# Strassen-like pairs in a two-layer encoder: block sums laid side by side, another order of a pair's products, block sums behind evacuations

## The chip, the cores and the metric

The kernel runs on one core of one Trainium2 chip. The metric is the device time of one execution in microseconds. Three runs of the kernel before have a median of 1820.8 us (1817.36 to 1824.54).

## The reference

A trunk of two layers over a sequence of 512 rows with 1024 channels, in float32. Each layer adds half a SwiGLU block, a mixer, and half a SwiGLU block again:

```python
h = _rmsnorm(x, ffn1_norm[layer])
x = x + 0.5 * _swiglu(h, ffn1_w_gate[layer], ffn1_w_up[layer], ffn1_w_down[layer])
...
def _swiglu(h, w_gate, w_up, w_down):
    return (jax.nn.silu(h @ w_gate) * (h @ w_up)) @ w_down
```

The hidden width of a SwiGLU block is 2816. The mixer of the first layer is a state-space mixer beside an S5 scan, that of the second banded attention beside causal pooling. The four SwiGLU blocks (f0 to f3) are most of the work, and the change is in them.

## The kernel before, in words

**Layout and stages.** Channels lie on the 128 partitions, the 512 rows of the sequence on the free axis. The program goes f0, even mixer, f1, f2, odd mixer, f3. Each float32 product is made from split operands: a matrix is split into a rounded part and a rest (`split_steps`, L582: ScalarE writes the rounded part, VectorE the rest), and three products (rounded x rounded, rounded x rest, rest x rounded) add up in one PSUM bank.

**Classic tiles and pairs.** The 22 output tiles of the gate matrix and of the up matrix go two by two (q = 0 to 10). Up to q = 7 in f0, and up to q = 1 in f1, f2 and f3, they are computed one tile after another ("classic"), with an evacuation (`evac`) by VectorE for each. From there on a pair of tiles is computed with seven block products instead of eight, after Winograd's form of Strassen's method (`pair`, L924): six pairs in f0 and 18 in each other stage, 60 in all; one half for the gate matrix (tag gs), one for the up matrix (tag us). A pair needs combinations of its weights (W1, W3, W4, W2; made by the feeder, `feed`, L508, on VectorE as raw<-raw sums and then split into whl and wh) and combinations of the normed activations, the block sums TA and TB (`blocks`, L876). The block sums are made once a stage: four steps, each with two normed tiles, four differences of 256 columns, and two splits into hg tiles.

**The products of a pair.** `block` (L904) runs four contraction steps into one bank. A narrow block has three products of 256 columns per step. A wide block (with TA at hi, or TB) has per step one product of 512 columns, which reads the rounded and the rest part of a block sum in one instruction, and one of 256. The two parts lie 512 elements apart in the tile, since each tile is [rounded 512 | rest 512] and a block takes columns lo (0 to 255) or hi (256 to 511) of both. A pair has three banks: X (W1 with N), Z (W4 with N, then W3 with TA), Y (W3 with TA, then W4 with TB, then W2 with TB). The last block, W2, is run later by `last()`: after the down products that follow the pair, or inside the next pair where none follow (`before`, the first pairs of f1, f2 and f3). Banks come from a pool of four that are used in turn.

**VectorE in a pair.** It reads X as p (p1), adds Y's two halves and p into the result tile (`plus`: gs<-ps,p then gs<-ps,gs), adds Z, and so on. The result tile gs or us is a single buffer: `ftile` (L842) waits until the gate of the tiles before (`gate`, L976: us<-gs,us and two splits) has issued its product. Y's bank gets its second group of products only when `plus` of the first has read it.

**What sets the order.** The order of all instructions is fixed when the program is built, by a planner: `Clock` (L111) keeps an estimated time for each engine and adds the cost of every instruction (`cost`, L145; for VectorE 0.068 us and 1/960 or 1/1920 us per element). Every few products `tick` (L285) offers a step first to urgent work, then to the feeder of weights, then to threads in order of `PRIO` (L58): a step for VectorE is issued when its operands are nearly ready and VectorE's estimated queue is less than BACKLOG beyond now (`on`, L320). Evacuations, gates and block sums have priority 0, the preparation of the S5 tables in f0 has 6. Waiting (`until`, `idle`) goes on ticking with no product issued.

Of the kernel before, what the change touches and what calls it, by code (L numbers as in the profile page):

```python
# [14 lines left out]
PSUM = bass.MemoryType.PSUM  # L15
# [17 lines left out]
for _i, _pools in enumerate(((),(3,),(2,),(1,0))):  # L33
# [21 lines left out]
WARM = 12  # L55
SLACK = {"f0": 1.5, "even": 0.0, "f1": 0.0, "f2": 0.0, "odd": 0.4, "f3": 0.0}
PREP_SLACK = 4.0
PRIO = {"evac": 0, "gate": 0, "small": 5, "prep": 6, "blocks": 0, "s5_bounce": 1, "s5_quarter": 0, "s5_gate": 0, "s5_eighth": 1,  # L58
        "ssd_dt": 1, "conv": 1, "ssd_chunk": 1, "ssd_tail": 0, "z": 2, "qk_norm": 0, "pool": 3, "attn": 2}
LIVE = 3  # L60
CHAINS = 2
# [49 lines left out]
class Clock:  # L111


    def __init__(self):
        self.t = dict.fromkeys(list(ENGINES.values()) + ["RING", "DMA"], 0.0)
        self.t["ACT"], self.t["RING"], self.t["DVE"], self.t["PE"] = 1.9, 0.65, 0.6, 0.95
        self.w, self.r, self.floor, self.stuck = {}, {}, 0.0, 0
        self.lanes, self.born = [0.0] * 8, {}

    @property  # L120
# [24 lines left out]
    def cost(eng, op, out, kw):  # L145
# [12 lines left out]
        ptr = any(hasattr(kw.get(k), "space") for k in ("scalar", "scalar1"))  # L158
        return (0.128 if ptr else 0.068) + n / (1920 if one else 960) * (1 if eng == "DVE" else 2)

    def note(self, eng, op, args, kw):
        out = kw.get("out", args[0] if args else None)
        outs = [out] + ([kw["accum_out"]] if "accum_out" in kw else [])
        ins = [v for k, v in kw.items() if k not in ("out", "accum_out") and hasattr(v, "free_size")]
        dma = op == "dma_start"
        at = self.t["RING"] if dma else self.t[eng]
        for ap in ins:
            for b in self.blocks(ap):
                t, e = self.w.get(b, (0.0, ""))
                at = max(at, t + (0.15 if e != eng else 0.11 if eng != "PE" else 0.0))  # L170
        for ap in outs:
            at = max(at, self.born.get(ap.name, 0.0))
            for b in self.blocks(ap):
                t, e = self.w.get(b, (0.0, ""))
                at = max(at, 0.0 if dma and e == "DMA" else t if e == eng else t + 0.1, self.r.get(b, 0.0))
        if dma and eng == "POOL":
            self.t["POOL"] = max(at, self.t["POOL"]) + 1.1
            end = max(self.t["DMA"], self.t["POOL"] + 1.0) + max(0.18, out.free_size() * out.partition_size() * 4 / 360e3)
            self.t["DMA"] = end
            end += 0.95  # L180
        elif dma:
            at = max(at, self.lanes.pop(0))
            self.t["RING"] = at + 0.48
            end = max(self.t["DMA"], at + 1.1) + max(0.06, out.free_size() * out.partition_size() * 4 / 360e3)
            self.t["DMA"] = end
            end += 1.06
            self.lanes.append(end)
        else:
            end = at + self.cost(eng, op, out, kw)
            self.t[eng] = end  # L190
        for ap in outs:
            for b in self.blocks(ap):
                self.w[b] = (max(end, self.w.get(b, (0.0, ""))[0]), "DMA" if dma else eng)
        for ap in ins:
            for b in self.blocks(ap):
                self.r[b] = max(self.r.get(b, 0.0), end)
# [55 lines left out]
class Builder:  # L252
# [26 lines left out]

    def phase(self, name):  # L280
        self.name = name
        self.backlog, self.guard, self.most = BACKLOG[name], GUARD[name], AHEAD[name]


# [296 lines left out]

    def split_steps(self, src, dst, scale=None):  # L582
        nc = self.nc
        yield from self.on("ACT", src)
# [4 lines left out]
        yield from self.on("DVE", dst[:, 0])  # L589
# [158 lines left out]
    def ffn(self, f, gi, then, prepare=None):  # L748
        nc, tc = self.nc, self.tc
        self.phase(f"f{f}")  # L750
        self.f, self.then, self.final, self.sideb = f, then, False, 2
        h = self.begin_norm(gi)
        with ExitStack() as st:
            self.ft = st.enter_context(tc.tile_pool(name=self.n("ft"), bufs=2))
            ex = ExitStack()
            prep = None
            if prepare is not None:
                prep = prepare(ex.enter_context(tc.tile_pool(name=self.n("prep"), bufs=1)))
# [11 lines left out]
            self.N, self.TA, self.TB = h, [], []  # L770
            grown, pending = False, None
            for key in ffn_items(f):
                if not grown and not self.running(prep) and CLASSIC[f == 0] < NFF // 2:
# [8 lines left out]
                if key[0] != "wgu":  # L782
                    w = self.unit(*key)
                if key[0] == "wgu":
                    m, i = key[2:]
                    if (m % 2, i) == (0, 0):
                        t, done = {"gs": None, "us": None}, []
                    if (m, i) == (0, 0):
                        both = self.proj_tiles([key, ("wgu", f, 0, 1)], h)
                    if m == 0:  # L790
                        ps = both[i]
                    else:
                        w = self.unit(*key)
# [7 lines left out]
                elif key[0] == "pair":  # L801
                    q, i = key[2:]
                    if i == 0:
                        t = {}
                    last = self.pair(w, t, "us" if i else "gs", pending)

                    def pending(last=last, t=t, q=q, i=i):
                        last()
                        if i == 0:
                            nc.scalar.activation(out=t["gs"], in_=t["gs"], func=AF.Silu)  # L810
                        else:
                            self.add("gate", self.gate(t, g, q, [1] * 4, 1))
                            if q == NFF // 2 - 1:
                                self.give(*self.N, *self.TA, *self.TB)
                else:
                    cg, kp = key[2:]
                    grp = next(gr for gr in GROUPS if kp in gr)
                    if kp == grp[0]:
                        pss = [None] * 4
                        if cg == 0 and grp == GROUPS[-1]:  # L820
                            self.tail()
                    self.out_unit(pss, w, g, kp, cg, kp == grp[0], kp == grp[-1], 0.5, "a")
                    self.give(w)
                    if cg == 1:
                        self.give(g[2 * kp], g[2 * kp + 1])
                    if pending:
                        pending()
                        pending = None
# [47 lines left out]
    def blocks(self, h, gi, late):  # L876
# [5 lines left out]
        for kk in range(4):  # L882
# [11 lines left out]
            v.tensor_tensor(out=t4, in0=n2[:, a], in1=t2, op=ALU.subtract)  # L894
            self.give(tn)
            for c, d in ((lo, self.TA), (hi, self.TB)):
                t = yield from self.grab("hg")
                yield from self.split_steps(rt[:, c], t)
                d.append(t)
            self.give(rt)  # L900
        self.xhold, self.reserve = False, 0


    def block(self, ps, t, at, rhs, c, more=False, wide=False):  # L904
        nc = self.nc
        for kk in range(4):
            self.until(lambda: len(rhs) > kk)
            w = slice(at + kk * P, at + kk * P + P)
            r = rhs[kk]
            first, last = kk == 0 and not more, kk == 3  # L910
            o = ps[:, 0:256]
            go = dict(start=first, stop=False, skip_group_check=more)
            if wide:
                nc.tensor.matmul(out=ps.rearrange("p (a b) -> p a b", a=2), lhsT=t[:, 0, w], rhs=r[:, :, c], **go)
            else:
                nc.tensor.matmul(out=o, lhsT=t[:, 0, w], rhs=r[:, 0, c], **go)
                go["start"] = False
                nc.tensor.matmul(out=o, lhsT=t[:, 0, w], rhs=r[:, 1, c], **go)
            nc.tensor.matmul(out=o, lhsT=t[:, 1, w], rhs=r[:, 0, c], start=False, stop=last, skip_group_check=more)
            self.tick()  # L920


# [1 line left out]
    def pair(self, w, t, tag, before):  # L924
        v = self.nc.vector
        W1, W3, W4, W2 = w
# [13 lines left out]
        self.block(X, W1, 0, N[0:4], lo)  # L940
        p1 = new("p1", 2)
        times(p1, X[:, lo], lo)
        Z = self.main_ps()
        self.block(Z[:, hi], W4, 512, N[4:8], hi)
        if before:
            before()
        t[tag] = dst = self.ftile(tag)
        Y = self.main_ps()
        self.block(Y, W3, 512, TA, hi, wide=wide)
        plus(dst[:, 0, hi], Y, p1)  # L950
        self.block(X, W1, 512, N[4:8], lo, more=True)
        self.give(W1)
        times(dst[:, 0, lo], X[:, lo], lo)
        self.free(X)
# [12 lines left out]

        def last():
            self.block(Y, W2, 0, TB, hi, more=True, wide=wide)
            self.give(W2)  # L970
            plus(dst[:, 1, lo], Y, p1)
            self.free(Y)
# [1120 lines left out]
```

## Time and profile before

| | |
|---|---|
| median of three runs | 1820.8 us |
| the profiled execution | 1818.1 us, its span 1816.4 us |
| TensorE products | 10082, busy 99% of the span |
| VectorE | 2902 instructions, busy 84% |
| ScalarE | 1032 instructions, busy 41% |
| granted TensorE clock, mean | 0.999 |

All rows have the same source line, that of a helper which records each operation (L207), so groups are told apart by the tiles they write and read: ps is a PSUM bank, whl and wh are split weights, hg a split activation or block sum, raw an unsplit weight or sum. "A<-B 128x512 xN | busy, mean" is a group of N instructions with its busy time in us and the mean of one in ns; what follows is the idle time of the engine ahead of them and who ended it. PEld is the loading of weights into TensorE, which carries the waits of the product behind it. Products are pipelined: the busy times of neighbours overlap, so the distance of their starts is what one costs.

### The profile page before, as it was taken

The numbers are of one execution on the slowest core, as the hardware profiler recorded it, in microseconds if no ns is written. First come the engines' busy times: TensorE is split into PE (matmuls) and PEld (weight loads), VectorE is DVE, ScalarE is ACT, GpSimd is POOL, SyncE is SP. The second block draws the span as 40 slices with busy tenths as digits, with TensorE's granted clock in tenths as the row PEclk, the third lists the DMA queues.
The fourth block names the chain that finished last, engine by engine and source line by source line (L and its number), as shares of the span: only waits on it lengthen the run. The fifth ranks groups of instructions, "written<-read, shape, count | busy, mean of one in ns | idle before, by whom it ended". The sixth has DMA issues, their size and how long they took to land.

```text
span 1816.4 us, 26183 instructions
## 1 busy us (share of the span) xinstructions
PE 1790.0 (99%) x10082; PEld 1535.7 (85%) x10082; DVE 1518.7 (84%) x2902; ACT 746.4 (41%) x1032; POOL 34.0 (2%) x53
## 2 busy tenths in 40 slices
PE   9999999999999999999999999999999999999999
PEld 7877888878778888888888898988888888988887
DVE  8999878777885899998779998987678679999984
ACT  4224433233584533333354333323466564333331
POOL 0000000000010000000010000000000010000000
PEclk9999999999999999999999999999999999999999
DMA  5256433336674532333343333333325452333331
GB/s 194 88 152 194 130 93 93 116 136 196 173 181 139 127 107 96 101 104 107 126 119 102 105 105 105 105 106 115 111 82 116 129 134 87 105 105 104 106 103 71
DMA packets 83341, 216.57 MB, mean 119 GB/s; under 512 B 18288, under 2 KB 30608, under 8 KB 82064
## 3 DMA queue, kind: packets, MB, share of 16 engines
q1 hardware_dynamic: 78032, 196.52, 33.7%
q0 software_dynamic: 5040, 18.35, 6.0%
q8 instruction: 79, 1.29, 0.3%
q14 instruction: 46, 0.38, 0.1%
q10 hardware_dynamic: 144, 0.02, 0.0%
HBM read 202.26 MB, written 12.60 MB: 118 GB/s over the span
## 4 chain that ended last, share of the span: by engine, by line
PE 64%; DVE 23%; DMA 6%; issue 4%; ACT 3%; SPq 0%; DVEq 0%; ACTq 0%
PE ps L207 64%; DVE whl L207 5%; DVE raw L207 4%; DVE us L207 4%; DMA raw<-in_wgu_dram 3%; ACT whl L207 2%; DVE gs L207 2%; DVE hg L207 2%; DVE x L207 1%; DVE wh L207 1%; DVE p L207 1%; DMA raw<-in_wev_dram 0%; DMA prm<-prm 0%; SPq L207 0%; DMA hg<-s5us 0%
## 5 line engine op out<-in xcount | busy, mean ns | idle before, releaser
L207 PE MATMUL ps<-hg,whl 128*128 128x512 f32 (+1 forms) x8400 | 1596.6, 349 | 12.4 <-DVE gs L207 6.1
L207 PEld LDWEIGHTS ps<-hg,whl 128*128 128x128 f32 x8400 | 1341.3, 189 | 221.4 <-DVE gs L207 10.8
L207 ACT CAST whl<-raw 128x1024 fp32r<-128x1024 f32 x374 | 391.1, 1048 | 500.9 <-PE ps L207 356.1
L207 DVE TENSOR_TENSOR whl<-raw,whl 128x1024 fp32r<-128x1024 f32 x339 | 412.2, 1219 | 100.6 <-ACT whl L207 100.3
L207 DVE TENSOR_TENSOR raw<-raw,raw 128x512 f32<-128x512 f32 (+1 forms) x212 | 129.5, 646 | 2.5
L207 ACT CAST hg<-us 128x512 fp32r<-128x512 f32 x88 | 52.0, 618 | 156.1 <-DVE us L207 155.9
L207 ACT ACTIVATE gs<-gs 128x1024 f32<-128x1024 f32 x44 | 46.6, 1060 | 159.9 <-DVE gs L207 159.9
L207 DVE SCALAR_TENSOR_TENSOR x<-ps,x 128x512 f32<-128x512 f32 x128 | 83.4, 683 | 19.3 <-PE ps L207 19.3
L207 PE MATMUL ps<-hg,wh 128*128 128x512 f32 x480 | 94.2, 339 | 0.9 <-DVE gs L207 0.9
L207 PEld LDWEIGHTS ps<-hg,wh 128*128 128x128 f32 x480 | 77.2, 188 | 13.8 <-DVE gs L207 1.6
L207 DVE TENSOR_TENSOR raw<-raw 128x512 f32<-128x512 f32 (+1 forms) x92 | 54.7, 595 | 19.0 <-DMA raw<-in_wgu_dram 18.4
L207 DVE TENSOR_TENSOR gs<-ps,gs 128x256 f32<-128x256 f32 x150 | 63.5, 424 | 4.1
L207 DVE TENSOR_TENSOR us<-ps,us 128x256 f32<-128x256 f32 x150 | 63.5, 423 | 4.1
L207 DVE TENSOR_TENSOR hg<-us,hg 128x512 fp32r<-128x512 f32 x88 | 59.2, 684 | 2.8 <-ACT hg L207 2.7
L207 DVE TENSOR_TENSOR us<-ps,p 128x256 f32<-128x256 f32 x90 | 37.8, 420 | 26.4 <-PE ps L207 26.2
L207 DVE TENSOR_TENSOR us<-gs,us 128x1024 f32<-128x1024 f32 x44 | 53.7, 1220 | 0.8
L207 DVE TENSOR_TENSOR p<-ps,rsB 128x256 f32<-128x256 f32 x120 | 49.9, 416 | 0.0
L207 ACT ACTIVATE hg<-x,gains 128x512 fp32r<-128x512 f32 x48 | 33.6, 720 | 31.2 <-DVE x L207 28.6
L207 DVE TENSOR_TENSOR gs<-ps,p 128x256 f32<-128x256 f32 x90 | 37.8, 420 | 8.7 <-PE ps L207 6.9
L207 DVE TENSOR_TENSOR us<-ps,rsB 128x512 f32<-128x512 f32 (+1 forms) x62 | 36.0, 581 | 6.3 <-PE ps L207 6.2
L207 DVE TENSOR_TENSOR wh<-raw,wh 128x512 fp32r<-128x512 f32 x60 | 41.0, 684 | 0.0
L207 DVE SCALAR_TENSOR_TENSOR hg<-x,gains,hg 128x512 fp32r<-128x512 f32 x48 | 35.5, 746 | 5.7 <-ACT hg L207 5.7
(258 smaller groups left out, 1083.4 us busy)
## 6 DMA issues: line engine op xcount, KB each, us to landing
raw<-in_wgu_dram SPq DMA_DIRECT2D x176, 512.0 KB, 3.5
raw<-in_wdn_dram SPq DMA_DIRECT2D x88, 512.0 KB, 4.1
whl<-in_wgu_dram POOLq DMA_DIRECT2D x18, 512.0 KB, 6.7
raw<-in_wev_dram SPq DMA_DIRECT2D x16, 512.0 KB, 4.1
prm<-prm SPq DMA_DIRECT2D x8, 1024.0 KB, 6.9
raw<-in_wod_dram SPq DMA_DIRECT2D x12, 512.0 KB, 3.5
raw<-in_wevo_dram SPq DMA_DIRECT2D x8, 512.0 KB, 6.9
raw<-in_wodo_dram SPq DMA_DIRECT2D x8, 512.0 KB, 6.6
```

Of the source, the lines that this page charges most:

```text
L207: r = f(*args, **kw)
```

## The change

Four edits.

1. The block sums' tiles get another layout: for the lo and for the hi half, the rounded part and the rest lie side by side (256 and 256), so that the wide product's moving operand is one run of 512 elements. The splits write two runs of 256.
2. In a pair, Z's products with W4 come behind Y's with W3 where no block of the pair before is pending, and Z's with W3 ahead of X's second group everywhere.
3. The priority of the block sums goes from 0 to 1.
4. In stage f0 the planner charges VectorE 0.09 us for an instruction whose operands start at other partitions than those before, and a little more for a reciprocal. No instruction is added by this.

```diff
-PRIO = {"evac": 0, "gate": 0, "small": 5, "prep": 6, "blocks": 0, "s5_bounce": 1, ...
+PRIO = {"evac": 0, "gate": 0, "small": 5, "prep": 6, "blocks": 1, "s5_bounce": 1, ...
...
+    def moved(self, ins, out):
+        at = lambda ap: (ap.space == PSUM, ap.start_partition() // 32)
+        held = any(self.reads.get(m, q) != q for m, q in map(at, ins))
+        m, q = at(out)
+        held = held or self.writes.get(m, q) != q
+        self.writes[m] = q
+        for m, q in map(at, ins[::-1]):
+            self.reads[m] = q
+        return 0.09 if held else 0.0
...
+            if eng == "DVE" and self.fine:
+                end += self.moved([ap for ap in ins if ap.free_size() > 1], out)
+                if op == "reciprocal":
+                    end += out.free_size() * 0.005
...
+        self.clk.fine = name == "f0"
...
                 t = yield from self.grab("hg")
-                yield from self.split_steps(rt[:, c], t)
-                d.append(t)
+                tv = t.rearrange("p a b -> p (a b)").rearrange("p (c j b) -> p j c b", c=2, j=2)
+                yield from self.split_steps(rt[:, c].rearrange("p (c b) -> p c b", c=2), (t, tv))
+                d.append(tv)
+                self.TS.append(t)
...
         self.block(X, W1, 0, N[0:4], lo)
         p1 = new("p1", 2)
         times(p1, X[:, lo], lo)
-        Z = self.main_ps()
-        self.block(Z[:, hi], W4, 512, N[4:8], hi)
         if before:
+            Z = self.main_ps()
+            self.block(Z[:, hi], W4, 512, N[4:8], hi)
             before()
         t[tag] = dst = self.ftile(tag)
         Y = self.main_ps()
-        self.block(Y, W3, 512, TA, hi, wide=wide)
+        self.block(Y, W3, 512, TA, 1, wide=wide)
         plus(dst[:, 0, hi], Y, p1)
+        if not before:
+            Z = self.main_ps()
+            self.block(Z[:, hi], W4, 512, N[4:8], hi)
+        self.block(Z, W3, 0, TA, 0)
+        self.give(W3)
+
+        add(dst[:, 0, hi], Z[:, lo], dst[:, 0, hi])
+        p5 = new("p5", 1)
+        times(p5, Z[:, hi], hi)
+        add(dst[:, 0, hi], dst[:, 0, hi], p5)
         self.block(X, W1, 512, N[4:8], lo, more=True)
         self.give(W1)
         times(dst[:, 0, lo], X[:, lo], lo)
         self.free(X)
-        self.block(Z, W3, 0, TA, lo)
-        self.give(W3)
-
-        add(dst[:, 0, hi], Z[:, lo], dst[:, 0, hi])
-        p5 = new("p5", 1)
-        times(p5, Z[:, hi], hi)
-        add(dst[:, 0, hi], dst[:, 0, hi], p5)
-        self.block(Y, W4, 0, TB, lo, more=True, wide=wide)
+        self.block(Y, W4, 0, TB, 0, more=True, wide=wide)
```

More of the change, by code (lines that the diff above doesn't have):

```diff
@@ L57 @@
 PREP_SLACK = 4.0
-PRIO = {"evac": 0, "gate": 0, "small": 5, "prep": 6, "blocks": 0, "s5_bounce": 1, "s5_quarter": 0, "s5_gate": 0, "s5_eighth": 1,
+PRIO = {"evac": 0, "gate": 0, "small": 5, "prep": 6, "blocks": 1, "s5_bounce": 1, "s5_quarter": 0, "s5_gate": 0, "s5_eighth": 1,
         "ssd_dt": 1, "conv": 1, "ssd_chunk": 1, "ssd_tail": 0, "z": 2, "qk_norm": 0, "pool": 3, "attn": 2}
@@ L117, in __init__ @@
         self.w, self.r, self.floor, self.stuck = {}, {}, 0.0, 0
+        self.reads, self.writes, self.fine = {}, {}, True
         self.lanes, self.born = [0.0] * 8, {}
@@ L583, in split_steps @@
         nc = self.nc
+        whole, dst = dst if isinstance(dst, tuple) else (dst[:, 0], dst)
         yield from self.on("ACT", src)
@@ L588, in split_steps @@
             nc.scalar.activation(out=dst[:, 0], in_=src, func=AF.Copy, scale=scale)
-        yield from self.on("DVE", dst[:, 0])
+        yield from self.on("DVE", whole)
         if scale is None:
@@ L769, in ffn @@
             g, pss = [None] * NFF, None
-            self.N, self.TA, self.TB = h, [], []
+            self.N, self.TA, self.TB, self.TS = h, [], [], []
             grown, pending = False, None
@@ L813, in pending @@
                             if q == NFF // 2 - 1:
-                                self.give(*self.N, *self.TA, *self.TB)
+                                self.give(*self.N, *self.TS)
                 else:
@@ L905, in block @@
         nc = self.nc
+        o = ps[:, 0:256]
         for kk in range(4):
@@ L908, in block @@
             w = slice(at + kk * P, at + kk * P + P)
[L909 to L912, printed above, removed]
+            r = [rhs[kk][:, j, c] for j in range(2)]
+            go = dict(start=kk == 0 and not more, stop=False, skip_group_check=more)
             if wide:
-                nc.tensor.matmul(out=ps.rearrange("p (a b) -> p a b", a=2), lhsT=t[:, 0, w], rhs=r[:, :, c], **go)
+                nc.tensor.matmul(out=ps.rearrange("p (a b) -> p a b", a=2), lhsT=t[:, 0, w], rhs=rhs[kk][:, :, c], **go)
             else:
-                nc.tensor.matmul(out=o, lhsT=t[:, 0, w], rhs=r[:, 0, c], **go)
+                nc.tensor.matmul(out=o, lhsT=t[:, 0, w], rhs=r[0], **go)
                 go["start"] = False
-                nc.tensor.matmul(out=o, lhsT=t[:, 0, w], rhs=r[:, 1, c], **go)
-            nc.tensor.matmul(out=o, lhsT=t[:, 1, w], rhs=r[:, 0, c], start=False, stop=last, skip_group_check=more)
+                nc.tensor.matmul(out=o, lhsT=t[:, 0, w], rhs=r[1], **go)
+            nc.tensor.matmul(out=o, lhsT=t[:, 1, w], rhs=r[0], start=False, stop=kk == 3, skip_group_check=more)
             self.tick()
@@ L948, in pair @@
         Y = self.main_ps()
-        self.block(Y, W3, 512, TA, hi, wide=wide)
+        self.block(Y, W3, 512, TA, 1, wide=wide)
         plus(dst[:, 0, hi], Y, p1)
[L951 to L954, printed above, removed]
-        self.block(Z, W3, 0, TA, lo)
+        if not before:
+            Z = self.main_ps()
+            self.block(Z[:, hi], W4, 512, N[4:8], hi)
+        self.block(Z, W3, 0, TA, 0)
         self.give(W3)
@@ L961, in pair @@
         add(dst[:, 0, hi], dst[:, 0, hi], p5)
-        self.block(Y, W4, 0, TB, lo, more=True, wide=wide)
+        self.block(X, W1, 512, N[4:8], lo, more=True)
+        self.give(W1)
+        times(dst[:, 0, lo], X[:, lo], lo)
+        self.free(X)
+        self.block(Y, W4, 0, TB, 0, more=True, wide=wide)
         self.give(W4)
@@ L968, in last @@
         def last():
-            self.block(Y, W2, 0, TB, hi, more=True, wide=wide)
+            self.block(Y, W2, 0, TB, 1, more=True, wide=wide)
             self.give(W2)
```

## The prediction

> **What bounds the kernel now.** I read the page first, then the matmul groups with their shapes kept apart, then the waits of TensorE's weight loads stage by stage, and the timelines of TensorE and VectorE around some of these waits.
>
> ```profile
> span 1816.4 us, 26183 instructions
> PE 1790.0 (99%) x10082; PEld 1535.7 (85%) x10082; DVE 1518.7 (84%) x2902; ACT 746.4 (41%) x1032; POOL 34.0 (2%) x53
> ...
> PE 64%; DVE 23%; DMA 6%; issue 4%; ACT 3%; SPq 0%; DVEq 0%; ACTq 0%
> ```
>
> TensorE is busy nearly all of the time and carries 64% of the chain; VectorE carries 23%, the places where TensorE waits for it. So time can come from two sources only: cheaper products, and fewer of these waits. How far apart products start is what counts, since their busy times overlap:
>
> ```profile
> L207 PE MATMUL ps<-hg,whl 128*128 128x512 f32 x5040 | 1251.3, 393 | 11.8 <-DVE gs L207 6.1 <-DVE hg L207 1.6 <-DVE us L207 1.4
> L207 PE MATMUL ps<-hg,whl 128*128 128x256 f32 x3360 | 489.7, 283 | 0.6 <-DVE p L207 0.6
> L207 PE MATMUL ps<-hg,wh 128*128 128x512 f32 x240 | 87.3, 398 | 0.9 <-DVE gs L207 0.9
> ```
>
> Their starts are in TensorE's timeline, two answers of it:
>
> ```profile
> 1085.69 5.16 PE L207 MATMUL ps<-hg,whl 128*128 128x512 f32 x22
> 1091.83 0.87 PE L207 MATMUL ps<-hg,wh 128*128 128x512 f32 x4
> 1092.54 2.80 PE L207 MATMUL ps<-hg,whl 128*128 128x256 f32 x22
> ```
>
> The first and third of the timeline rows are a stretch of one kind of product each. A down product (512 columns in one run) starts (5.16 - 0.393)/21 = 0.227 us after the one before it, a 256-column product (2.80 - 0.283)/21 = 0.120 us. The row between them is two wide products of a pair, which read two runs of 256, and two of 256 columns: from 1091.83 to the next group's start are 0.71 us, so a wide one takes (0.71 - 0.24)/2 = 0.235 us.
>
> **Part 1: sums side by side.** It removes no product; it makes the moving operand of each wide product one run of 512. There are 240 with wh as weights, four for each of 60 pairs, and eight more per pair (W3, W4) among those with whl: 720 in all. If they cost what the down products cost, 720 x 8 ns = 5.8 us go. The resolution of the rows (0.01 us over two products) allows 3 to 13 ns; I take the 8. Part of it falls where TensorE is not the bound:
>
> ```profile
> 596.00:628.00 32.00, 32.00 (x143) 26.50 (x142) 30.65 (x54) 17.84 (x23) 2.55 (x3) 1.00 0.51 130
> 628.00:665.00 37.00, 36.23 (x242) 33.01 (x241) 36.20 (x62) 15.66 (x19) 0.00 (x0) 1.00 0.27 88
> 665.00:976.00 311.00, 309.25 (x1785) 272.75 (x1784) 267.49 (x451) 122.47 (x147) 5.12 (x6) 1.00 0.36 110
> ```
>
> In the columns (us, PE, PEld, DVE) VectorE fills 36.2 of 37 us at the first three pairs of f1, against 86% of the stretch behind. The code is the same in f2 and f3, so I leave out nine pairs, 9 x 12 x 8 ns = 0.9 us. **Part 1: 4.9 us less**, between 0 and 5.8.
>
> The Trainium skill (Advanced Engine Details and Errata, Memory Cachelines) says that accesses which hit the same 16-byte line again run at full speed. By that a break every 256 elements costs nothing, and this part would give 0 instead of 4.9 us. The 8 ns above speak against it; it is the third rival.
>
> **Part 2: the order in a pair.** Now it is X (N low), Z (W4), Y (W3), X again, Z again, Y (W4). New, where no product of the pair before is pending: X, Y, Z, Z, X, Y. Y's second group still starts after the same 56 products, but 36 narrow ones (36 x 0.120 = 4.3 us) instead of 24 (2.9 us) stand between it and the end of Y's first. It needs that the two additions which read Y ("plus") are done. These waits show in the weight loads:
>
> ```profile
> PEld ps L207 <- DVE p L207: 1.2, 2, 0.6
> PEld ps L207 <- DVE gs L207: 0.7, 2, 0.4
> PEld ps L207 <- DVE gs L207: 2.6, 4, 1.2
> PEld ps L207 <- DVE gs L207: 2.1, 4, 0.9
> PEld ps L207 <- DVE gs L207: 2.2, 4, 0.7
> ```
>
> The rows are of 254 to 360 us (f0's pairs), 628 to 665, and the late pairs of f1, f2 and f3: 6.9 us in twelve waits there. That looks like a gain of 6.9 us. I doubt it because of what VectorE does before these additions:
>
> ```profile
> 1092.95 0.41 DVE L207 TENSOR_TENSOR us<-ps,p 128x256 f32<-128x256 f32 x1
> 1093.40 0.42 DVE L207 TENSOR_TENSOR us<-ps,us 128x256 f32<-128x256 f32 x1
> 1093.74 0.68 DVE L207 TENSOR_TENSOR raw<-raw 128x512 f32<-128x512 f32 x1
> 1094.46 1.90 DVE L207 TENSOR_TENSOR raw<-raw,raw 128x512 f32<-128x512 f32 x3
> 1096.28 0.42 DVE L207 TENSOR_TENSOR p<-ps,rsB 128x256 f32<-128x256 f32 x1
> 1096.61 1.22 DVE L207 TENSOR_TENSOR whl<-raw,whl 128x1024 fp32r<-128x1024 f32 x1
> 1097.74 1.22 DVE L207 TENSOR_TENSOR us<-gs,us 128x1024 f32<-128x1024 f32 x1
> 1099.06 0.42 DVE L207 TENSOR_TENSOR gs<-ps,p 128x256 f32<-128x256 f32 x1
> 1099.52 0.42 DVE L207 TENSOR_TENSOR gs<-ps,gs 128x256 f32<-128x256 f32 x1
> ```
>
> Y's second group was due about 1099.7 (X started at 1092.54; 48 narrow and 8 mixed products are 48 x 0.120 + 4 x 0.355 = 7.2 us) and the additions ended at 1099.94. VectorE did not idle before them waiting for Y: it worked without a gap through p, a weight split and the last gate's product us. The tile gs cannot be taken before that gate product has been issued (the pair waits for room at once after X in the new order), and the feeder of weights comes ahead of the gate in every tick. So split and gate product stay ahead of the additions, and they end when they did. I keep the 6.9 us. What goes is the wait for p in f0, of which the later wait for Y takes most back, and short waits where nothing was forced ahead. **Part 2: 1 us less**; the ends are 1 us more (new waits of the same kind) and 6.9 + 1.2 = 8.1 us less. Weights are given back as before: one after the 44th product, one after the 56th.
>
> **Part 3: VectorE's cost in the planner, f0 only.** No instruction is added; the order in which f0 issues them changes. The planner charges a copy of 32 elements 0.068 + 32/1920 = 0.085 us.
>
> ```profile
> L207 DVE COPY s5x<-s5pr 64x32 f32<-64x32 f32 x16 | 3.1, 193 | 0.2
> ```
>
> In the timeline, two of these copies and two that stay on all 128 partitions:
>
> ```profile
> 52.09 0.20 DVE L207 COPY s5x<-s5pi 64x32 f32<-64x32 f32 x1
> 52.30 0.19 DVE L207 COPY s5x<-s5a 64x32 f32<-64x32 f32 x1
> 76.97 0.20 DVE L207 COPY s5er<-s5cs 128x32 f32<-128x32 f32 x1
> 77.06 0.19 DVE L207 COPY s5ei<-s5sn 128x32 f32<-128x32 f32 x1
> ```
>
> Copies that change between partition halves start 0.21 us apart, those that do not 0.09. The 16 of the first row alone put VectorE 16 x 0.12 = 1.9 us behind the plan. What came of it: the weight loads' waits up to 240 us, TensorE's timeline around the longest, and the stretch behind it (PEclk is the third number from the end):
>
> ```profile
> PEld ps L207 <- DVE gs L207: 3.2, 2, 2.6
> PEld ps L207 <- ACT bl L207: 0.9, 1, 0.9
> 95.08 0.97 PE L207 MATMUL ps<-hg,whl 128*128 128x512 f32 x3
> 98.17 6.22 PE L207 MATMUL ps<-hg,whl 128*128 128x512 f32 x19 [2.12 <-DVE gs L207]
> 99.50:102.70 3.20, 3.20 (x9) 2.43 (x8) 3.00 (x17) 1.09 (x2) 0.00 (x0) 0.51 0.30 116
> ```
>
> At 95.08 + 3 x 0.227 = 95.76 TensorE was due with a product whose bank VectorE had not yet emptied of gs; it started at 98.17, 2.4 us late. Then its clock stood at 0.51 for 3.2 us: the 19 products took 6.22 - 0.39 = 5.83 us for 18 starts instead of 4.09, another 1.7 us. With 0.09 us charged per change the plan knows of the lag, holds the low-priority preparation back and issues the evacuation earlier. I expect these 4.1 us to go, and half of the 0.9 us of waiting for bl. **Part 3: 4.5 us less**, between 0 (another place takes the wait) and 6.
>
> By the Trainium skill (TensorE: Matmul & The Clock Gate, Part 1) the clock falls to half after an idle window of about 3.4 us. By that the half clock would not be the gap's doing and this part would give 2.4 + 0.4 = 2.8 us; the rows show it behind a gap of 2.1 us.
>
> **Part 4: block sums behind evacuations.** Around the end of the sums in f1:
>
> ```profile
> 624.16 1.29 DVE L207 TENSOR_TENSOR hg<-raw,hg 128x512 fp32r<-128x512 f32 x2
> ...
> 631.36 0.42 DVE L207 TENSOR_TENSOR p<-ps,rsB 128x256 f32<-128x256 f32 x1
> ```
>
> The last sum lands at 625.45. The first pair's X ends about 2 us before its p is taken at 631.36 (p was that late above: 1092.54 + 12 x 0.120 = 1094.0 against 1096.28), and Y, which needs the sums, now follows at once: 3.9 us of cover. An evacuation covers 512 columns, 0.68 us by the raw row above, and most of the eight already stand ahead. **0**, and 1 us either way.
>
> The splits into the new tiles also write two runs of 256 instead of one of 512: 32 on VectorE and as many on ScalarE, all ahead of the pairs. The dearest view of two runs is two instructions of 256 at 0.42 us against one of 512 at 0.68: 0.16 us a piece, covered by the classic tiles' products, and 8 x 0.16 = 1.3 us a stage if that cover were gone.
>
> The sum is 4.9 + 1 + 4.5 = 10.4 us. The profiled execution took 1818.1 us (span 1816.4 and 1.7 around it), so 1807.7 for it; the three runs have a median of 1820.8, so **1810.4**.
>
> **The rivals.** First: the additions do come earlier, because the reordered issue puts them ahead of the weight split, and the waits of the pairs go: 7.1 us more, 1803.3. For it: 1.4 us more distance, and every one of the twelve waits is at most 1.2 us. Against: VectorE's gapless row of work. Second: f0's gap moves instead of going; part 3 is 0, 1814.9. For it: VectorE's work is the same, and it is dense there (3.00 of 3.20 us). Third: one run costs what two did, 1815.3. Fourth, slower: a new wait in the bank. Four banks turn; with X, Y, Z in this order, Z gets the bank of the Y of the pair before, which frees when the additions behind W2 are done. Place: Z's first product, X and Y after W2, 12 x 0.120 + 4 x 0.347 = 2.8 us behind it, in some 54 pairs. Above, these additions ended at 1093.82, 1.3 us behind 1092.54. Each further lag beyond 2.8 us costs once per pair: at 0.5 us 27 us, 1837. It decides for slower from 0.36 us on the mean (54 x 0.36 = 19.5 us eats the gain and 9.1 more). Against it: half of the margin is free in the row.
>
> **Numbers.** The forecast has 0.48, the rivals 0.22, 0.17, 0.08 and 0.05. About 0.5%, 9.1 us, is what a measurement of this kernel can tell from no change. The forecast's 10.4 us lie just past it: with its unknowns 0.33 of its 0.48 is faster; with nearly all of the first rival and a little of the second and third that is 0.55. Slower is the fourth, 0.05; the rest, 0.40, is no difference. The range is 1800 to 1818: the first rival with the upper ends, and the second with part 1 at half.
>
> **What would show it.** Right: the 398 ns of wh's 128x512 products fall to the 393 of the others; no clock of 0.5 between 90 and 110 us; the weight loads still wait for gs in the pairs, some 7 us. Wrong: these waits vanish (first rival), a gap over 2 us stays in f0 (second), weight loads wait for us at Z (fourth). A longer first pair in f1 would show part 4 as a cost.

## The result, and the profile after

The changed kernel takes **1810.5 us** (median of 5 runs, 1807.42 to 1812.46) against 1820.8 us before (median of 5 runs, 1817.36 to 1824.54): a ratio of 0.9943, 95% interval 0.9925 to 0.996. That is 10.3 us less. The two profiled executions are closer together than the medians, 1818.1 us before and 1812.5 us after, since the first lies low among the runs of its kernel and the second is the longest of its own.

The page of the kernel after, the lines that answer to those of before (the helper that records every instruction is now line 223):

```profile
PE 1787.6 (99%) x10082; PEld 1536.4 (85%) x10082; DVE 1518.0 (84%) x2902; ACT 744.5 (41%) x1032; POOL 33.9 (2%) x53
...
PE 75%; DVE 15%; DMA 5%; issue 2%; ACT 2%; SPq 1%; DVEq 0%; ACTq 0%
```

No engine has less work. What changed is the chain: VectorE carries 15% of it instead of 23%. So most of the gain lies in waits. The matmul groups, shapes apart:

```profile
L223 PE MATMUL ps<-hg,whl 128*128 128x512 f32 x5040 | 1250.8, 394 | 3.0 <-DVE hg L223 1.6 <-DVE whl L223 1.0 <-ACT whl L223 0.3
L223 PE MATMUL ps<-hg,whl 128*128 128x256 f32 x3360 | 489.8, 283 | 2.4 <-DVE gs L223 2.4
L223 PE MATMUL ps<-hg,wh 128*128 128x512 f32 x240 | 87.3, 398 | 1.1 <-DVE gs L223 1.1
```

The first row had 11.8 us of idle time, 6.1 of it for gs; now it has 3.0 and none for gs. The second row is worse, 2.4 us for gs against 0.6 for p. The third row, the wide products with wh, still has 398 ns: the one run of 512 columns did not make them cheaper. The weight loads' waits, first of the stretch from 628 to 665 us, then of the late pairs of f2 (the row of f3 is the same):

```profile
PEld ps L223 <- issue: 1.0, 1, 1.0
PEld ps L223 <- DVE gs L223: 0.6, 1, 0.6
...
PEld ps L223 <- DVE gs L223: 0.2, 1, 0.2
```

The pairs of f0 (254 to 360 us) and the late pairs of f1 (665 to 976 us) show no wait at all. Of the 6.9 us before, 0.4 us are left in the late pairs of f2 and f3. New is a pair of waits, 1.0 and 0.6 us, at the second pair of f1, f2 and f3. They make these stretches longer by 0.3 us at most: before, the same stretch of f1 had waits of 0.7 us for gs and 0.7 us for us, and that of f2 1.0 and 0.7 us. In TensorE's timeline the new waits are these:

```profile
639.34 1.67 PE L223 MATMUL ps<-hg,whl 128*128 128x256 f32 x12 [0.81 <-DVE gs L223]
641.36 1.68 PE L223 MATMUL ps<-hg,wh 128*128 128x512 f32 x8 [0.36 <-DVE gs L223]
```

The first row is Z of the stage's second pair, the second the pending product (W2) of the first pair. VectorE's timeline has the read-out of X of the pair before just ahead, from 638.77 to 639.19:

```profile
638.77 0.42 DVE L223 TENSOR_TENSOR gs<-ps,rsB 128x256 f32<-128x256 f32 x1
```

Z takes the bank that this frees. The planner's part of f0 is the other place that I had counted on. TensorE's timeline there:

```profile
98.75 4.60 PE L223 MATMUL ps<-hg,whl 128*128 128x512 f32 x19
...
125.15 0.42 PE L223 MATMUL ps<-g,s5bm 128*32 128x128 f32 x8 [1.29 <-ACT bl L223]
...
141.27 0.66 PE L223 MATMUL ps<-ident,bt 128*128 128x128 f32 x4 [1.18 <-DVE bt L223]
...
171.24 0.66 PE L223 MATMUL ps<-ident,bt 128*128 128x128 f32 x4 [0.75 <-DVE bt L223]
```

The gap ahead of 98 us and the half clock behind it are gone (18 starts in 4.21 us, 0.234 us each). In their place stand three waits of 1.29, 1.18 and 0.75 us (before, TensorE waited 0.7 us for bl and 0.4 us for bt). The products with wh are the last block of a pair, in both orders, so the first and the last start in their row bound the pairs. Before, then after:

```profile
L207 PE MATMUL ps<-hg,wh x480: 277/336/504, 268.3 to 1790.4; 128*128 128x512 f32 x80, 128*128 128x256 f32 x80
```

```profile
L223 PE MATMUL ps<-hg,wh x480: 277/336/501, 267.8 to 1784.7; 128*128 128x512 f32 x80, 128*128 128x256 f32 x80
```

The first came 0.5 us earlier, the last 5.7 us, which is this profile's gain. Read product by product from the two traces, from a stage's first pair to its last block with wh, the pairs of f0 are shorter by 1.0 us, those of f1 by 2.4, of f2 by 1.9 and of f3 by 1.8: 7.0 us in all. What lies between the pairs of f0 and of f1 is 1.9 us longer; after, two stretches at half the granted clock fell into it (from 457.7 and from 543.0 us), before none.

The medians differ by more, 10.3 us. A part of that is clock: the mean granted clock on record is 0.9975 over 71 runs of the kernel before and 0.9989 over ten of the kernel after, and 0.0014 of 1815 us is 2.5 us, an estimate that takes TensorE for the bound all the time. With the 7.0 us in the pairs that is most of the 10.3 us.

**Why the additions are no longer late.** I had worked through the pair at 1092 us. The same pair after, first TensorE (pending W2, then X), then VectorE:

```profile
1089.10 1.56 PE L223 MATMUL ps<-hg,wh 128*128 128x512 f32 x8
1090.50 10.83 PE L223 MATMUL ps<-hg,whl 128*128 128x256 f32 x73
```

```profile
1084.90 0.68 DVE L223 TENSOR_TENSOR wh<-raw,wh 128x512 fp32r<-128x512 f32 x1
1085.50 0.42 DVE L223 TENSOR_TENSOR us<-ps,p 128x256 f32<-128x256 f32 x1
...
1093.60 0.42 DVE L223 TENSOR_TENSOR p<-ps,rsB 128x256 f32<-128x256 f32 x1
1093.93 1.22 DVE L223 TENSOR_TENSOR whl<-raw,whl 128x1024 fp32r<-128x1024 f32 x1
1095.06 1.22 DVE L223 TENSOR_TENSOR us<-gs,us 128x1024 f32<-128x1024 f32 x1
1096.38 0.42 DVE L223 TENSOR_TENSOR gs<-ps,p 128x256 f32<-128x256 f32 x1
1096.84 0.95 DVE L223 TENSOR_TENSOR gs<-ps,gs 128x256 f32<-128x256 f32 x2
```

X starts at 1090.50, so Y's second group is due at 1097.7 (7.2 us later, as before). The two additions that read Y end at about 1096.84 + 0.42 = 1097.3: in time by 0.4 us, where they were 0.2 us late. The split and the gate product still stand ahead of them, just as I said; but p is taken 3.10 us behind X's start, not 3.74. The 0.64 us are, up to 0.04 us, one weight split, wh. Before, VectorE did it behind the previous pair's additions:

```profile
1087.57 0.42 DVE L207 TENSOR_TENSOR us<-ps,p 128x256 f32<-128x256 f32 x1
...
1089.42 0.68 DVE L207 TENSOR_TENSOR wh<-raw,wh 128x512 fp32r<-128x512 f32 x1
```

Now it does it ahead of them (1084.90, before us<-ps,p at 1085.50). The split takes 0.60 us of VectorE's queue, and in this pair that is the difference.

The twelve late pairs are not all like this one. Three of them are, one at the same place in each of f1, f2 and f3. In three more the split stays where it was, and p comes 0.2 to 0.5 us earlier. The other six, toward the end of each stage, hold the five longest waits. In the longest, at 839 us, VectorE did idle behind p (838.47 us), for a weight's transfer, and then made four weight sums:

```profile
839.68 0.69 DVE L207 TENSOR_TENSOR raw<-raw 128x512 f32<-128x512 f32 x1 [0.80 <-DMA raw<-in_wgu_dram]
840.41 1.90 DVE L207 TENSOR_TENSOR raw<-raw,raw 128x512 f32<-128x512 f32 x3
```

After, wh has moved ahead in these six too, VectorE does not idle behind p, and two of the four sums stand ahead of p (839.08 us):

```profile
837.75 0.68 DVE L223 TENSOR_TENSOR raw<-raw 128x512 f32<-128x512 f32 x1
838.46 0.69 DVE L223 TENSOR_TENSOR raw<-raw,raw 128x512 f32<-128x512 f32 x1
```

Here p is later behind X's start than before, and yet the additions are in time. Four of the six had such an idle time before (0.80, 0.51, 0.30 and 0.30 us). That the moved split is what ends it was not tested.

### The profile page after: what moved, and what is told of

It reads as the page before. It is cut to its first block, busy times and chain, and to the rows that moved or that the text cites. A ratio compares the mean times of both kernels' runs of the same rounds, so it can differ in the third digit from the quotient of the medians.

```text
span 1810.8 us, 26209 instructions
## 1 busy us (share of the span) xinstructions
PE 1787.6 (99%) x10082; PEld 1536.4 (85%) x10082; DVE 1518.0 (84%) x2902; ACT 744.5 (41%) x1032; POOL 33.9 (2%) x53
## 3 DMA queue, kind: packets, MB, share of 16 engines
q8 instruction: 79, 1.29, 0.3%
## 4 chain that ended last, share of the span: by engine, by line
PE 75%; DVE 15%; DMA 5%; issue 2%; ACT 2%; SPq 1%; DVEq 0%; ACTq 0%
PE ps L223 75%; DVE whl L223 3%; DMA raw<-in_wgu_dram 2%; DVE hg L223 2%; DVE raw L223 2%; DVE us L223 1%; ACT whl L223 1%; DVE gs L223 1%; SPq L223 1%; DVE ct L223 1%; DVE ex L223 1%; DMA prm<-ct 1%; DVE g L223 0%; DMA prm<-prm 0%; DMA raw<-in_wev_dram 0%
## 5 line engine op out<-in xcount | busy, mean ns | idle before, releaser
L223 ACT ACTIVATE whl<-raw 128x1024 fp32r<-128x1024 f32 x35 | 36.9, 1056 | 8.1 <-PE ps L223 5.1
```

What stands on the lines that cost most here:

```text
L223: r = f(*args, **kw)
```

## The experiments

All are the kernel before or after with the edit shown. The kernel before ran beside them on the same chip each time; its median was 1820.7 us beside the first four, 1820.4 beside the next four and 1820.0 beside the last four.

**Each part alone.** The order of the products alone (the whole of the change to the pair's function, no more):

```
-        Z = self.main_ps()
-        self.block(Z[:, hi], W4, 512, N[4:8], hi)
...
+        if not before:
+            Z = self.main_ps()
+            self.block(Z[:, hi], W4, 512, N[4:8], hi)
```

> Only the new order of the products in a pair; layout, priority and planner as before. Theory: the order alone takes the waits at Y's second group away (the weight loads' waits for gs in the late pairs of f1, f2 and f3 fall from 6.9 us in twelve to under 1 us) and alone brings a wait of about 1 us at Z in the second pair of each of these stages, where X is read out later and Z takes its bank: 6 to 8 us less in all. Rival: the waits went because the evacuations pass the block sums; then the order alone leaves the 6.9 us, and the time is within 2 us of before.

Measured: 1823.0 us, ratio 1.0016 (1.0008 to 1.0025). My theory fell: alone, the order that I held for the source of the gain makes the kernel slower. The late pairs of f1 and f2 do lose their waits, those of f3 fall from 2.2 to 1.3 us. The wait at Z, which I had expected from the order, is not there. But in the third pair of each stage Y's second group waits, longer than any wait in the kernel before. TensorE in f1's third pair, then VectorE there:

```profile
657.68 4.65 PE L207 MATMUL ps<-hg,whl 128*128 128x512 f32 x21 [2.50 <-DVE gs L207]
```

```profile
651.38 0.42 DVE L207 TENSOR_TENSOR us<-ps,us 128x256 f32<-128x256 f32 x1
651.74 0.69 DVE L207 TENSOR_TENSOR raw<-raw 128x512 f32<-128x512 f32 x1
652.47 1.90 DVE L207 TENSOR_TENSOR raw<-raw,raw 128x512 f32<-128x512 f32 x3
654.28 1.22 DVE L207 TENSOR_TENSOR whl<-raw,whl 128x1024 fp32r<-128x1024 f32 x1
655.41 1.22 DVE L207 TENSOR_TENSOR us<-gs,us 128x1024 f32<-128x1024 f32 x1
656.74 0.42 DVE L207 TENSOR_TENSOR gs<-ps,p 128x256 f32<-128x256 f32 x1
```

Four weight sums (raw) and a split stand between the last addition into us and the gate product us<-gs,us, and so ahead of the additions into gs. In the kernel after the same place reads:

```profile
653.66 0.42 DVE L223 TENSOR_TENSOR us<-ps,us 128x256 f32<-128x256 f32 x1
654.12 1.23 DVE L223 TENSOR_TENSOR us<-gs,us 128x1024 f32<-128x1024 f32 x1
655.26 0.68 DVE L223 TENSOR_TENSOR raw<-raw 128x512 f32<-128x512 f32 x1
655.86 0.42 DVE L223 TENSOR_TENSOR gs<-ps,p 128x256 f32<-128x256 f32 x1
```

The gate product comes at once, and the additions 2.2 us after us<-ps,us has started instead of 5.36 us. In the order-only kernel's profile the granted clock also falls to half behind two of the three waits (0.53 from 1008.3 to 1011.7 us); its mean over the runs is 0.9956.

The layout alone (the indices in the pair's function go with it):

```
-                t = yield from self.grab("hg")
-                yield from self.split_steps(rt[:, c], t)
-                d.append(t)
+                t = yield from self.grab("hg")
+                tv = t.rearrange("p a b -> p (a b)").rearrange("p (c j b) -> p j c b", c=2, j=2)
+                yield from self.split_steps(rt[:, c].rearrange("p (c b) -> p c b", c=2), (t, tv))
+                d.append(tv)
```

> Only the block sums' layout. Theory: a wide product of one run still starts 0.235 us ahead of the next, as with two runs, so the time is that of before within 1 us. Rival: one run costs 0.227 us and the gain was lost elsewhere in the changed kernel: 4 to 6 us less.

Measured: 1818.9 us, ratio 0.9994 (0.9985 to 1.0002), nothing that can be told from no change.

The planner's charge alone (moved(), its use for VectorE in f0 and the little more for a reciprocal, nothing else):

```
+            if eng == "DVE" and self.fine:
+                end += self.moved([ap for ap in ins if ap.free_size() > 1], out)
```

> Only the planner's charge for VectorE in f0. Theory: the gap of 2.4 us at 98 us and the half clock behind it go, two or three smaller waits (1.4, 1.0, 0.6 us) come at 120 to 175 us, f0 is 0.5 to 2 us shorter, and nothing changes behind f0. Rival: f0's gain is 4 us and more, and the changed kernel lost it to the block sums' priority.

Measured: 1819.4 us, ratio 0.9997 (0.9988 to 1.0005). The gap at 98 us goes, as in the kernel after, and other waits take its place. A row of the weight loads' waits up to 240 us:

```profile
PEld ps L222 <- DVE bt L222: 3.4, 3, 1.6
```

The kernel before had 3.2 us there for gs and none for bt; here 1.2 us for gs are left. By the profiles, what the charge saves is the half clock rather than the gap. The order-only kernel still has the gap (2.14 us at 98.17 us) but a full clock behind it, and its first pair starts at 253.7 us, as in the kernel with the charge alone (253.7) and in the kernel after (253.8), against 254.3 us before.

The priority alone:

```
-PRIO = {"evac": 0, "gate": 0, "small": 5, "prep": 6, "blocks": 0, ...
+PRIO = {"evac": 0, "gate": 0, "small": 5, "prep": 6, "blocks": 1, ...
```

> Only the block sums' priority. Theory: no effect, within 1 us; no wait at Z in the second pairs. Rival: it is this edit that delays the second pairs: about 1 us a stage, 3 us more in all.

Measured: 1822.1 us, ratio 1.0008 (0.9999 to 1.0018), the wrong side of no difference. The wait at the second pair, which I had not expected from this part, comes with it, for p in place of gs, and large in f2 only (0.2 and 0.3 us for p in f1 and f3). In f2 it is

```profile
986.68 3.53 PE L207 MATMUL ps<-hg,whl 128*128 128x256 f32 x17 [2.11 <-DVE p L207]
```

By their medians the four parts alone add up to +2.3 - 1.8 - 1.2 + 1.4 = +0.7 us. Together they give -10.3. So the gain is in a combination.

**Order and priority together.** Both edits above on the kernel before, no layout, no planner charge.

> The kernel before with two parts of the change, the order of the products in a pair and the block sums' lower priority; layout and planner charge stay as before. Theory (the two parts need each other: the new order removes the waits for Y, and the lower priority keeps the weight split from going ahead of the last gate product and the additions in the third pair of a stage): nearly the whole gain, 8 to 10 us less than the kernel before, 1811 to 1813 us; the three waits of 2.6 to 2.8 us at Y's second group in the third pair, which the order alone showed, are gone; a wait of about 1 us at Z in the second pair stays. Rival (the gain needs layout or planner charge as well, or is spread evenly over three of them): within 4 us of the kernel before, 1817 to 1822 us, and the waits of 2.6 us are still there.

Measured: 1812.8 us, ratio 0.9962 (0.995 to 0.9975): 7.6 us less, though each of the two alone is no gain. VectorE in the third pair of f1 has the kernel after's order again, the gate product ahead of the weight sums:

```profile
654.59 1.22 DVE L207 TENSOR_TENSOR us<-gs,us 128x1024 f32<-128x1024 f32 x1
655.73 0.68 DVE L207 TENSOR_TENSOR raw<-raw 128x512 f32<-128x512 f32 x1
```

The theory held: 1812.8 us lies in its 1811 to 1813, the gain just below its 8 to 10 us, and the waits of 2.6 us are gone while those of the second pair stay.

**The kernel after without the layout:** all but the edit shown for the layout.

> The kernel after without the sums side by side: new order, lower priority and planner charge, the sums in two runs of 256. Theory (the layout gives nothing): within 1 us of the kernel after. Rival (the layout gives up to 2 us once the waits are gone): 1812 to 1813 us.

Measured: 1809.9 us, ratio 0.9947 (0.9934 to 0.9959). The kernel after, run once more beside it,

> The kernel after once more, on the same chip as the three others, for the differences of 1 to 4 us. Every theory expects 1809.5 to 1811.5 us; half clock stretches of 3.4 us at other places than in its first profile.

took 1810.2 us (0.9949, 0.9936 to 0.9961). The layout gives nothing with the waits gone either. This kernel differs from the one with order and priority alone by the planner's charge only: 0.9947 against 0.9962, 2.7 us, with intervals that overlap. So the charge may be worth more here than the 0.0003 it gave alone; the times do not settle it. The clocks on record fit: 0.9974 in the five runs without the charge, 0.9990 in the five with it, and 0.0016 of 1811 us is 2.9 us, an estimate by which the whole difference could be time at half clock. In the pairs the kernel with order and priority alone already is 6.5 us shorter than the kernel before, of the 7.0 us of the kernel after.

**The bank for Z.** In the kernel after:

```
         if before:
-            Z = self.main_ps()
+            Z = self.main_ps("a")
```

> The kernel after, but Z of the pairs with pending products gets its bank from the other group of four, the one of the classic tiles and the down products. Theory (Z in the second pair of f1, f2 and f3 waits for the bank of the pair before, whose X is read out late): the three waits of about 1 us go, and the half clock that can follow one; 3 us less than the kernel after, about 1807 us. Rival (the wait only moves on to the next product that needs the same VectorE instructions, in the second or third pair): no difference, within 1 us of the kernel after.

Measured: 1818.0 us, ratio 0.9991 (0.9982 to 1.0): 7.5 us slower than the kernel after. The rival was nearer, and too mild. In f2:

```profile
989.49 1.68 PE L223 MATMUL ps<-hg,wh 128*128 128x512 f32 x8 [1.42 <-DVE gs L223]
...
1010.57 3.69 PE L223 MATMUL ps<-hg,whl 128*128 128x512 f32 x15 [1.47 <-DVE gs L223]
```

Z no longer waits, but the pending W2 behind it now waits 1.42 us in place of 0.36, for the same VectorE work. And the borrowed bank is missed: the down products behind the third pair wait 1.47 us for it. The same wait stands at 661.29 us in f1. From the stage's first pair to the third's last block each of f1, f2 and f3 is 1.7 to 1.9 us longer than in the kernel after, 5.4 us in all.

**Wide products in a group.** One run of 512 between narrow products takes the 0.235 us that two runs took, while the down products take 0.227. In the kernel after, each wide block issues its four wide products and then its four narrow ones:

```
+        if wide:
+            for half in range(2):
+                for kk in range(4):
...
+                    if half == 0:
+                        nc.tensor.matmul(out=ps.rearrange("p (a b) -> p a b", a=2), lhsT=t[:, 0, w], rhs=rhs[kk][:, :, c],
...
+                    else:
+                        nc.tensor.matmul(out=o, lhsT=t[:, 1, w], rhs=rhs[kk][:, 0, c], start=False, stop=kk == 3,
...
+            return
```

> The kernel after, but each wide block issues its four wide products one after another and then its four narrow ones, in place of wide and narrow in turn; the sums are the same, in another order. Theory (the 8 ns by which a wide product is slower than a down product come from the alternation of 512 and 256 columns, since one run of 512 costs the same 235 ns as two runs did): 227 ns for a wide product, 720 x 8 ns = 5.8 us less than the kernel after, about 1805 us; at least 3 us if one of the four still pays for the change of width. Rival (the 8 ns belong to these operands or to their place in the bank): the wide product stays at 235 ns, the time within 1 us of the kernel after.

Measured: 1822.4 us, ratio 1.0014 (1.0005 to 1.0023), 11.9 us slower than the kernel after. Yet the products did get cheaper:

```profile
L223 PE MATMUL ps<-hg,wh 128*128 128x512 f32 x240 | 64.9, 392 | 3.4 <-DVE us L223 2.3 <-DVE gs L223 1.1
```

392 ns instead of 398. What costs is VectorE's order in the third pair, which has fallen back to that of the order alone:

```profile
651.40 1.90 DVE L223 TENSOR_TENSOR raw<-raw,raw 128x512 f32<-128x512 f32 x3
...
654.35 1.22 DVE L223 TENSOR_TENSOR us<-gs,us 128x1024 f32<-128x1024 f32 x1
```

TensorE waits 2.48 us for it at 656.61. The same kernel with the sums in two runs as before (the layout edit taken back):

> As the grouped kernel, but with the two parts of the sums as before the change, in two separate runs of 256 columns. Theory (two runs cost nothing at any place): the same time as the grouped kernel within 1 us, and the same spacing of the wide products. Rival (two runs cost 8 ns each, and in the kernel before this was hidden below the cost of the alternation): 5.8 us more than the grouped kernel, 235 ns for a wide product.

Measured: 1823.5 us, ratio 1.0019 (1.001 to 1.0028), and the same 64.9 us and 392 ns for the products with wh. Two runs cost nothing in a group either.

**Grouped, with VectorE's order kept.** Only Y's first group and W2 grouped (wide=2 stands for the branch above); this leaves VectorE's instructions in the order of the kernel after.

```
-        self.block(Y, W3, 512, TA, 1, wide=wide)
+        self.block(Y, W3, 512, TA, 1, wide=wide and 2)
...
-            self.block(Y, W2, 0, TB, 1, more=True, wide=wide)
+            self.block(Y, W2, 0, TB, 1, more=True, wide=wide and 2)
```

> The kernel after; only Y's first group (with W3) and the pending last group (with W2) issue their four wide products one after another and then the four narrow ones; Y's second group stays in turn. VectorE's instructions keep the order that they have in the kernel after. Theory (grouped wide products start 227 ns apart, as the first grouped kernel's trace showed, and that kernel lost only because the planner put a weight split ahead of the gate product again): six to seven of the eight products' 8 ns go in both blocks, 480 x 6 to 8 ns = 2.9 to 3.8 us less than the kernel after run beside it, and no wait of 2.6 us in the third pair. Rival (Y2 is then due earlier by as much, waits for the same additions, and the time stays): within 1 us of the kernel after, with 3 us more of waits at Y's second group.

Measured: 1808.3 us, ratio 0.9941 (0.9928 to 0.9955), 1.9 us less than the kernel after beside it. The intervals of the two overlap for the most part. The sign is the theory's, the size below its 2.9 us. The row and a W2 block with what follows it:

```profile
L223 PE MATMUL ps<-hg,wh 128*128 128x512 f32 x240 | 64.6, 391 | 1.1 <-DVE gs L223 1.1
```

```profile
1083.26 1.54 PE L223 MATMUL ps<-hg,wh 128*128 128x512 f32 x8
1084.63 7.55 PE L223 MATMUL ps<-hg,whl 128*128 128x256 f32 x57
```

The eight products take 1.37 us from start to start of the next, 1.40 in the kernel after (1089.10 to 1090.50): 0.03 us a block, 120 blocks, 3.6 us at that resolution. The single products in the trace are finer: a block with W2 falls from 1.400 to 1.379 us (medians), but from X's start to the end of Y's second group a pair falls only from 8.570 to 8.564 us. That is 27 ns for each of 60 pairs, 1.6 us, about what the time shows.

With Y's second group too, its narrow products first:

```
-        self.block(Y, W4, 0, TB, 0, more=True, wide=wide)
+        self.block(Y, W4, 0, TB, 0, more=True, wide=wide and 3)
```

> As the kernel before this one in the list, and Y's second group issues its four narrow products first and then the four wide ones. Some of VectorE's instructions change their order with it. Theory (distance to the additions): 240 x 6 to 8 ns = 1.4 to 1.9 us less than that kernel. Rival (the planner's order tips over again): waits of over 2 us at Y's second group, 3 us or more slower than that kernel.

Measured: **1806.7 us**, ratio 0.9929 (0.9917 to 0.9942), 3.5 us less than the kernel after beside it and 1.6 less than the one with two groups. It beats the kernel before; against the kernel after (0.9936 to 0.9961) the intervals just overlap. From X's start to the end of Y's second group a pair takes 8.563 us, so grouping this block makes it no cheaper. Where the 1.6 us would come from is open, and they are within the noise.

## Why the prediction was right, and which of its steps were wrong

The time came out as forecast, 1810.5 for 1810.4 us. The working did not: three of its four terms were wrong, in both directions, and their errors cancelled.

**Part 1, 4.9 us less: wrong, it is 0.** The failed step is "if they cost what the down products cost". The 8 ns of a wide product were there, but I put them down to the two runs of 256 because that was the one difference that the diff named. The wide products differ from the down products in a second thing: narrow ones stand between them. One run costs 398 ns as two did, and grouping takes it to 391. The term was also too large in itself. My row of 0.71 us was half of a block of eight; the whole took 1.40 us, because the narrow products between wide ones start after 0.116 us on the mean, not 0.120. Beside 4 x 0.347 us that leaves 3 ns for each wide product with wh, and 6 ns for those with W3 and W4 (1.411 us a block): 3.5 us in all, not 5.8. The zero was the third rival, to which I gave 0.08. The trace agrees here with the Trainium skill (Advanced Engine Details and Errata, Memory Cachelines), by which the break costs nothing; I had set its sentence aside for a row that could not tell the two causes apart.

**Parts 2 and 4, 1 us and 0: wrong, together they are 7.6 us.** The failed step is "so split and gate product stay ahead of the additions, and they end when they did". The first half is true of the pair that I worked through, the second is not: its additions end 0.64 us earlier, because another split (wh) has moved from behind the previous pair's additions to ahead of them. I looked at what stands directly before the late instruction and took the start of that row as fixed. I also took that pair for all twelve: "VectorE did not idle before them" fails for four of them, and in six the weight sums come forward as well. The waits stood on a lateness of 0.2 to 1.1 us, and 6.5 of their 6.9 us went. That is the outcome of the first rival, 0.22, though not by its reason: the additions do not pass the weight split. And "0, and 1 us either way" for the priority holds only beside the old order (+0.0008, within its interval); beside the new order it decides the sign, 1812.8 against 1823.0 us.

**Part 3, 4.5 us less: mis-sized.** The gap and the half clock went, as the rows said; three waits of 3.2 us in all came, which is the second rival's "gap moves". The wait for bl, which I had halved, grew: 1.7 us in the weight loads, not 0.9. In the profile 0.5 us are left at the end of this part, as much as the order-only kernel gains there by a full clock behind the same gap: the 2.4 us of the gap came to nothing. Against the kernel without the charge the part may be up to 2.7.

With the measured terms the sum is 0 + 7.6 + 2.7 = 10.3 us; it has to come out so, since the 2.7 are the difference of the kernels with and without the charge. That the time was met within 0.1 us is luck. The three rivals named one error each and I weighed them as if only one could hold. They held together: 1810.4 + 4.9 + 4.5 - 7.1 = 1812.7 us.

**The fourth rival** had the right resource, a bank at Z, at the wrong place. It does not strike the 54 pairs, but the second pair of each stage, where Z takes the bank of X, not of Y. By f1's waits, in three stages, it is 3 x 1.6 = 4.8 us of waiting, but other waits of 4.5 us went from the same three stretches, so the net cost is 0.5 us or less. Lending another bank costs more.

Of what was to show it: the clock between 90 and 110 us is full, as said. The 398 ns did not fall and the waits for gs did vanish, the two signs against parts 1 and 2. The first pair of f1 shows no cost of part 4; the second has the new waits.

What stays open: how the planner comes to put four weight sums ahead of the gate product in the third pair. The same order in the order-only kernel and the first grouped one, with the same wait of 2.5 us, shows that this order costs it; which of the planner's comparisons tips, no run shows.

## What to carry to other kernels

When TensorE waits a few tenths of a microsecond for a VectorE instruction at the end of a gapless row, follow that row back past its first idle time: one instruction of 0.6 us that moves to another place in the cycle can end the wait, and no look at the last four instructions tells it. Do so for more than one of the waits, since those that look alike can have different rows ahead of them. Where a planner orders the work, parts of a change are not additive: run the pairs of edits, not only each alone, and look for a wait that one of them adds in the first iterations of a stage. A spacing that differs between two groups of instructions is evidence for a cause only if the groups differ in that cause alone, and it is to be taken over a whole period, the neighbours included.

## What the runs showed of the hardware

**Alternation costs a little, runs do not.** A block of four wide products with wh and four narrow ones takes 1.400 us in turn, in one run or in two; grouped it takes 1.379 us, in one run or in two (398 against 391 to 392 ns in the rows). A block with W3 takes 1.411 us in turn and 1.401 grouped, again in one run or in two. Its wide products start 0.228 to 0.236 us apart even in a group, where those with wh start 0.227 us apart, so alternation explains only a part there; the rest is open.

**The half clock comes by chance behind short waits.** Ahead of a sum of squares (ysq) TensorE waits about as long in both kernels. Before, then after, with the 12 products that follow:

```profile
542.41 1.05 PE L207 MATMUL ps<-ones,ysq 128*128 128x1 f32 x8 [1.16 <-DVE ysq L207]
543.33 3.02 PE L207 MATMUL ps<-hg,whl 128*128 128x512 f32 x12
```

```profile
541.28 1.05 PE L223 MATMUL ps<-ones,ysq 128*128 128x1 f32 x8 [1.15 <-DVE ysq L223]
542.19 4.58 PE L223 MATMUL ps<-hg,whl 128*128 128x512 f32 x12
```

After the same wait the 12 products take 3.02 us in one profile and 4.58 in the other. The granted clock behind the wait in after (the third number from the end) is one half for 3.41 us:

```profile
543.00:546.41 3.41, 3.41 (x10) 2.64 (x9) 1.25 (x8) 0.00 (x0) 0.00 (x0) 0.51 0.96 190
```

Of the fourteen profiles eight have the half clock at this place and six have not. The gap of 2.1 us at 98 us had it behind it in four profiles of five. So 1.15 us of waiting, with eight products of one column behind it, can cost 1.6 us more, or nothing. This accounts for part of the spread between executions: the runs of the kernel before with a mean clock of 0.996 take 1822.1 us on the mean, those with 0.999 1818.2 us. The Trainium skill (TensorE: Matmul & The Clock Gate, Part 1) speaks of a free-running window of about 3.4 us; the length of the slow stretch agrees, but here a wait of a third of it stood ahead of it.
